# The shared keys by Strassen's seven products, in a float32 trunk of an mLSTM layer and a band-attention layer

## The chip, the cores and the metric

The kernel runs on one core of one Trainium2 chip. The metric is the device time of one execution in microseconds.

## The reference

512 tokens of width 2048 go through two layers. The first is an mLSTM mixer with eight heads, the second an attention mixer with sixteen heads of 128. Keys and values of the second layer are computed once, from the stream after the first layer:

```python
kmod = sc @ kv_ada_w.astype(F32) + kv_ada_b.astype(F32)
hkv = modulate(rmsnorm(x, kv_g), kmod[:, :D_MODEL], kmod[:, D_MODEL:]).astype(x.dtype)
kv = hkv @ kv_w
k_sh = kv[..., :B_WIDTH].reshape(Bn, S, B_HEADS, B_DH)
v_sh = kv[..., B_WIDTH:].reshape(Bn, S, B_HEADS, B_DH)
```

`hkv` is 512 x 2048, `kv_w` 2048 x 4096: one half of its columns gives the keys, the other the values. After that come the queries and a gate (`b_w_in`, 2048 x 4096), attention, and the output projection (`b_w_out`, 2048 x 2048). All is float32.

## The kernel before

Every float32 operand of a large product is held as a rounded half `hi` (type float32r) and a remainder `lo`. `split` makes them: ScalarE copies `hi` (line 153), VectorE subtracts for `lo` (line 154). A product of 128 x 128 weights with up to 512 tokens is then three matmuls, hi·hi, hi·lo, lo·hi (`mm3`); all of them are issued at line 174.

The weights lie in DRAM in the order in which they are used (`stream`). `wpiece` loads the next piece, as a rule 128 x 1024, into `wr` (tag `raw`, three buffers, line 167, on SP's queue like every DMA here) and splits it into `wh` and `wl` (three buffers each). From the end of the first stage on the pieces are issued with a priority of 300 instructions (`AHEAD`), so that they run ahead of the rest. The order on each engine and queue is fixed when the program is built: a list scheduler takes the ready instruction of the highest priority, and each engine then works in that order. A buffer is written again when its last reader is done.

`proj_a` makes one output tile of 128 columns by 512 tokens, with weights as the stationary operand: 16 k tiles, 48 matmuls, two pieces. `proj_b` makes tokens by 512 columns for several token tiles `m`, with the activations stationary.

The stages after the first layer are, in order:

- `rows`: the output projection of the first layer. Its input `y` is loaded from DRAM in pairs (`yr`, in the buffers of `raw`) and split (`y_tile`).
- `residual`, `turned`, `key_input`: the residual, its transposes (kept in DRAM in `nsc`), and `hkv` as hi and lo in the 16 buffers of `xp`.
- `values(g, ms)` for column groups 0 and 1, each for two pairs of token tiles (`PAIRS`). ScalarE copies the sums (`ps_kv`) to `kv[h]` in SBUF in pieces of 128 x 128 (line 685).
- The keys: 16 calls of `proj_a` with sums `ps_k`, copied to `kv[h]` (line 697).
- `values` for groups 2 and 3. While they run, `h2`, the input of the queries, is made from `nsc` into `xp` in place of `hkv`.
- Attention. Step `h` holds `queries(h)` (`ps_q`), `mixed(h - 2)` (`ps_o`), `weights(h - 1)` (`ps_s` and softmax), `gated(h)` (`ps_z`) and `flipped(h - 1)` (`ps_t`). `mixed` splits its output into `y2` in SBUF, in the buffers of `kp`.
- The output projection (`ps_y`), four column groups of `proj_b` over `y2`, and the last residual with `x2`, which is loaded into `xp` (line 813).

Of the kernel before, what the change touches and what calls it, by code (L numbers as in the profile page):

```python
# [9 lines left out]
F32 = mybir.dt.float32  # L10
# [5 lines left out]
P = 128  # L16
D = 2048
# [21 lines left out]
LATER += [DK, DK + P, V0 // 2 + DK, V0 // 2 + DK + P]  # L39


def stream():

    out = []

    def tile_a(mat, col, kts=KT):
        for k in range(0, kts, 8):
            out.append((mat, list(range(k, k + 8)), [(col, P)]))

    def tile_b(mat, col, kts=KT):  # L50
        for k in range(0, kts, 2):
            out.append((mat, [k, k + 1], [(col, 512)]))

    for k0, k1 in BLOCKS:
        for k in range(k0, k1):
            out.append(("a_w_in", [k], [(c, P) for c in LEAD]))
        for c in LATER:
            out.append(("a_w_in", list(range(k0, k1)), [(c, P)]))
    for h in range(NH):
        if h > 1:  # L60
            for c in (h * DK, h * DK + P, V0 // 2 + h * DK, V0 // 2 + h * DK + P):
                tile_a("a_w_in", c)
        tile_b("a_w_in", V0 + h * DV)
        if h:
            for c0 in (O0, Z0):
                for i in range(4):
                    tile_a("a_w_in", c0 + h * DV + i * P)
    tile_b("a_w_out", 0, 32)
    for _ in PAIRS:
        for g in range(1, 4):  # L70
            tile_b("a_w_out", g * 512, 32)
    for _ in PAIRS:
        for g in range(2):
            tile_b("kv_w", D + g * 512)
    for i in range(KT):
        tile_a("kv_w", i * P)
    for g in range(2, 4):
        tile_b("kv_w", D + g * 512)
    for h in range(BH):
        tile_a("b_w_in", h * P)  # L80
        tile_a("b_w_in", D + h * P)
    for g in range(3):
        tile_b("b_w_out", g * 512)
    for _ in PAIRS:
        tile_b("b_w_out", 3 * 512)
    return out


def sizes():
    return [len(kts) * sum(n for _, n in cs) for _, kts, cs in stream()]  # L90


CB = 0
# [12 lines left out]
def hybrid_trunk(ctx, tc, xT, xN, c, adaT, cols, wst, wg, ext, kc, out):  # L106
# [2 lines left out]

    const = ctx.enter_context(tc.tile_pool(name="const", bufs=1))  # L110
    dram = ctx.enter_context(tc.tile_pool(name="scr", bufs=1, space=bass.MemoryType.DRAM))
    wp = ctx.enter_context(tc.tile_pool(name="wp", bufs=3))
    xp = ctx.enter_context(tc.tile_pool(name="xp", bufs=KT))
    psP = ctx.enter_context(tc.tile_pool(name="psP", bufs=5, space=bass.MemoryType.PSUM))
    psA = ctx.enter_context(tc.tile_pool(name="psA", bufs=3, space=bass.MemoryType.PSUM))

    def pool(name, bufs=1):
        return tc.tile_pool(name=name, bufs=bufs, reuse_waits="tile")

    ysc = dram.tile([NH, P, 4, S], F32, name="ysc")  # L120
    gsc = dram.tile([2, NH, S], F32, name="gsc")
# [1 line left out]
    nsc = dram.tile([KT, P, S], F32, name="nsc")  # L123
    ggd = dram.tile([2, KT, P], F32, name="ggd")
    bsc = dram.tile([BH, P, EXTW], F32, name="bsc")

    cl = const.tile([P, NCOL], F32, name="cl")
    kcs = const.tile([P, 272], F32, name="kcs")
    ones_f = const.tile([P, P], F32, name="ones_f")
    ones_r = const.tile([P, P], F32R, name="ones_r")  # L130
# [8 lines left out]
    nc.vector.memset(ones_r.bitcast(F32), 1.0)  # L139
# [4 lines left out]
    maskd = kcs[:, 128:256]  # L144
    sel = kcs[:32, 256:272]

    def col(i):
        return cl[:, i : i + 1]
# [6 lines left out]

    ahead = [0]

    def wpiece(mat):

        i, at = wpos  # L160
        m, kts, cs = order[i]
        assert m == mat
        n = len(kts) * sum(w for _, w in cs)
        wpos[:] = i + 1, at + P * n
        with tc.high_priority(ahead[0]):
            raw = wp.tile([P, 1024], F32, tag="raw", name=f"wr{i}")[:, :n]
            nc.sync.dma_start(raw, wst[at : at + P * n].rearrange("(p n) -> p n", p=P))
            hi = wp.tile([P, 1024], F32R, tag="hi", name=f"wh{i}")[:, :n]
            lo = wp.tile([P, 1024], F32R, tag="lo", name=f"wl{i}")[:, :n]
            split(hi, lo, raw)  # L170
        return hi, lo

    def mm(ps, a, b, start, stop):
# [21 lines left out]
    def proj_b(mat, xs, pss, ms=range(4), kts=KT, at={}, late=0):  # L195


        held = []
        for k0 in range(0, kts, 2):
            if k0 in at:  # L200
                at[k0]()
            held.append((k0, *wpiece(mat)))
            if k0 >= kts - 2 * late and k0 < kts - 2:
                continue
            for group in [[pm] for pm in zip(pss, ms)] if k0 == kts - 2 else [list(zip(pss, ms))]:
                for ka, hi, lo in held:
# [7 lines left out]
            held.clear()  # L214

    def newp(name):
        return psP.tile([P, S], F32, tag="p", name=name)
# [46 lines left out]
    for q in range(4):  # L264
# [6 lines left out]
    pin(nc.sync.dma_start(kcs, kc))  # L271
# [63 lines left out]

    hp = hst.enter_context(pool("head"))
    aT = hp.tile([P, 4, NH], F32, name="aT")
    graw = tp.tile([P, KT, 16], F32, tag="t", name="graw")
    gw = hp.tile([P, KT, 32], F32R, tag="p0", name="gw")
    nc.sync.dma_start(graw, wg)  # L340
# [217 lines left out]

    kst = ExitStack()
    kp = kst.enter_context(pool("kp", bufs=KT))  # L560
    rst = ExitStack()
    rp = rst.enter_context(pool("rp", bufs=12))
    tst = ExitStack()
    tp = tst.enter_context(pool("t2", bufs=6))

    ys = []

# [107 lines left out]
            rows(g, ms, ys, at)  # L675


    kv = [kp.tile([P, 2, S], F32, tag="k", name=f"kv{h}") for h in range(BH)]
# [11 lines left out]
    for pair, ms in enumerate(PAIRS):  # L690
        for g in range(2):
            turn = {4 * i: lambda i=i: turned(1, [i], True) for i in range(4)} if pair == 0 and g == 1 else {}
            values(g, ms, turn)
    for i in range(KT):
        ps = newp(f"ps_k{i}")
        proj_a("kv_w", hkv, ps)
        nc.scalar.copy(kv[i][:, 0, :], ps)
    for g in range(2, 4):
        values(g, range(4))
    h2 = []  # L700
    for k in range(KT):
# [6 lines left out]
        h2.append(t)  # L708
    tst.close()
    rst.close()  # L710


    ast = ExitStack()
    at = ast.enter_context(pool("att"))
    y2 = []

    def queries(h):
        ps = newp(f"ps_q{h}")
        proj_a("b_w_in", h2, ps)
        q0 = at.tile([P, P], F32, tag="q0", name=f"q0_{h}")  # L720
# [71 lines left out]
    for h in range(BH + 2):  # L792
# [15 lines left out]
    yo = [[] for _ in range(4)]  # L808
    x2 = []
    for m in range(4):  # L810
        t = [xp.tile([P, 2, S], F32, tag="x", name=f"x2_{m}_{i}") for i in range(2)]
        for i in range(2):
            nc.sync.dma_start(t[i], xsc[m, :, 2 * i * S : 2 * (i + 1) * S].rearrange("p (a t) -> p a t", a=2))
        x2.append([t[g // 2][:, g % 2, :] for g in range(4)])

    def finish(m):
        rs = row_rstd(m)
# [5 lines left out]
    for g in range(4):  # L823
        gate_row(1, g)
        for pair in [range(4)] if g < 3 else PAIRS:
            ps = [newp(f"ps_y1_{g}_{m}") for m in pair]
            at = {4: lambda: finish(0), 6: lambda: finish(1)} if pair == PAIRS[1] else {}
            proj_b("b_w_out", y2, ps, ms=pair, at=at, late=3 if pair == PAIRS[1] else 0)
# [11 lines left out]
def layouts(x, c, ada_w, ada_b, g_pre, g_post, a_w_in, a_conv_w, a_conv_b, a_gate_b, a_g_head,  # L840
# [3 lines left out]
    def cc(v):  # L844
# [12 lines left out]
    order = stream()  # L857
    wst = np.concatenate(
        [
            np.concatenate([mats[mat][k * P : (k + 1) * P, c0 : c0 + n] for k in kts for c0, n in cs], 1).ravel()  # L860
            for mat, kts, cs in order
        ]
    )
    wg = np.ascontiguousarray(a_w_in[0][:, G0:].reshape(KT, P, 16).transpose(1, 0, 2))
# [3 lines left out]
    kc = np.zeros((P, 272), f)  # L868
    kc[:, :128] = np.eye(P)
    i = np.arange(P)  # L870
    kc[:, 128:256] = np.where(i[None, :] >= i[:, None], 0.0, NEG)
    kc[:32, 256:272] = np.tile(np.eye(16), (2, 1))
# [20 lines left out]
```

## Time and profile before

| | |
|---|---|
| time, median of 3 runs | 2862.86 us (2862.17 to 2864.84) |
| profiled execution, its own time | 2862.53 us |
| its span in the trace | 2860.7 us |
| granted TensorE clock | 0.999 |
| instructions | 33028 |
| matmuls | 12770 |

In the rows of the profile, PE is TensorE's matmuls and PEld its weight loads, DVE is VectorE, ACT is ScalarE, SP is the engine whose queue issues the DMAs, L174 is line 174. `ps_k<-hkv,wh` names what an instruction writes and reads. An arrow behind an idle time names what ended it.

### The profile page before, as it was taken

The page shows a single profiled execution, that of the slowest core. Times are in us where ns is not written, and L with a number is a line of the kernel's source. Part 1 is how long each engine was busy: PE and PEld are TensorE (multiplying, and loading weights), DVE is VectorE, ACT ScalarE, POOL GpSimd, SP SyncE. Part 2 cuts the span into 40 slices and gives each one's busy share as a digit, 9 for nine tenths or more (in the row PEclk, how much of TensorE's full clock was granted, in tenths as well). Part 3 has the DMA queues.
Part 4 walks back from the last instruction along what each step waited for, and adds up shares of the span by engine and source line. Part 5 has one row for each costly group of instructions (what it writes and reads, how often), then busy time and mean ns, then how long its engine had stood idle before and what let it go on. Part 6 is the DMA issues. An engine that isn't in the chain of part 4 may idle for free.

```text
span 2860.7 us, 33028 instructions
## 1 busy us (share of the span) xinstructions
PE 2832.2 (99%) x12770; PEld 2340.4 (82%) x12770; DVE 1587.4 (55%) x2358; ACT 1126.1 (39%) x1646; POOL 0.2 (0%) x4
## 2 busy tenths in 40 slices
PE   7999999999999999999999999999999999999998
PEld 5787888888888888888888888888888888888887
DVE  7986747466375564764735445575222455545425
ACT  4244524333242342332424345454222445545323
POOL 0000000000000000000000000000000000000000
PEclk9999999999999999999999999999999999999999
DMA  8874546456456464554635557786222322222334
GB/s 307 310 235 159 192 158 211 168 173 209 155 184 213 136 225 155 195 203 154 209 108 177 180 195 238 231 274 217 96 99 103 138 92 86 90 91 88 137 103 173
DMA packets 154950, 491.09 MB, mean 172 GB/s; under 512 B 17012, under 2 KB 26132, under 8 KB 154280
## 3 DMA queue, kind: packets, MB, share of 16 engines
q1 hardware_dynamic: 154792, 488.98, 50.2%
q8 instruction: 100, 1.64, 0.2%
q14 instruction: 58, 0.48, 0.0%
HBM read 467.89 MB, written 26.26 MB: 173 GB/s over the span
## 4 chain that ended last, share of the span: by engine, by line
PE 93%; DVE 3%; DMA 2%; issue 1%; ACT 1%; SPq 0%; DVEq 0%; ACTq 0%
PE ps_y L174 17%; PE ps_z L174 17%; PE ps_o L174 12%; PE ps_v L174 12%; PE ps_qk L174 9%; PE ps_q L174 6%; PE ps_k L174 6%; PE ps_kv L174 5%; PE ps_l L174 2%; PE ps_s L174 2%; PE ps_n L174 2%; PE ps_lead L174 1%; DVE wl L154 1%; DVE ada L245 1%; DMA wr<-in_wst 1%
## 5 line engine op out<-in xcount | busy, mean ns | idle before, releaser
L154 DVE TENSOR_TENSOR wl<-wr,wh 128x1024 fp32r<-128x1024 f32 (+3 forms) x586 | 680.4, 1162 | 1078.1 <-ACT wh L153 1077.6
L153 ACT CAST wh<-wr 128x1024 fp32r<-128x1024 f32 (+3 forms) x586 | 587.3, 1003 | 1433.0 <-PE ps_y L174 235.6
L174 PE MATMUL ps_y<-wh,y 128*128 128x512 f32 x1536 | 475.2, 390 | 0.0
L174 PE MATMUL ps_z<-h,wh 128*128 128x512 f32 x1408 | 433.9, 389 | 0.0
L174 PEld LDWEIGHTS ps_y<-wh,y 128*128 128x128 f32 x1536 | 288.2, 188 | 59.2
L174 PE MATMUL ps_v<-wh,h 128*128 128x512 f32 x1024 | 317.2, 389 | 0.0
L174 PEld LDWEIGHTS ps_z<-h,wh 128*128 128x128 f32 x1408 | 263.3, 188 | 54.0
L174 PE MATMUL ps_y<-wl,y 128*128 128x512 f32 x768 | 299.1, 389 | 0.0
L174 PE MATMUL ps_o<-h,wh 128*128 128x512 f32 x896 | 276.2, 389 | 0.0
L174 PE MATMUL ps_z<-h,wl 128*128 128x512 f32 x704 | 274.1, 389 | 0.0
L174 PE MATMUL ps_qk<-h,wh 128*128 128x512 f32 x768 | 237.8, 391 | 0.0
L174 PEld LDWEIGHTS ps_v<-wh,h 128*128 128x128 f32 x1024 | 192.1, 188 | 39.8
L174 PE MATMUL ps_v<-wl,h 128*128 128x512 f32 x512 | 199.4, 390 | 0.0
L174 PEld LDWEIGHTS ps_o<-h,wh 128*128 128x128 f32 x896 | 167.3, 188 | 34.1
L245 DVE CUSTOM_DVE_ANT_0 ada<-ada,scB,mod 128x1024 f32<-128x1024 f32 x128 | 164.1, 1282 | 24.2 <-DMA ada<-in_adaT 22.7
L174 PE MATMUL ps_o<-h,wl 128*128 128x512 f32 x448 | 174.4, 389 | 0.0
L174 PEld LDWEIGHTS ps_y<-wl,y 128*128 128x128 f32 x768 | 144.2, 188 | 30.0
L245 DVE CUSTOM_DVE_ANT_0 ada<-ada,scB,cl 128x1024 f32<-128x1024 f32 x128 | 164.0, 1282 | 6.0 <-DMA ada<-in_adaT 5.9
L174 PEld LDWEIGHTS ps_qk<-h,wh 128*128 128x128 f32 x768 | 143.2, 188 | 29.1
L174 PE MATMUL ps_q<-h,wh 128*128 128x512 f32 x512 | 159.3, 392 | 0.0
L174 PE MATMUL ps_kv<-wh,hkv 128*128 128x512 f32 x512 | 159.2, 391 | 0.0
L174 PE MATMUL ps_k<-hkv,wh 128*128 128x512 f32 x512 | 157.5, 389 | 0.0
(216 smaller groups left out, 3389.0 us busy)
## 6 DMA issues: line engine op xcount, KB each, us to landing
wr<-in_wst SPq DMA_DIRECT2D x520, 512.0 KB, 3.3
ada<-in_adaT SPq DMA_DIRECT2D x256, 512.0 KB, 5.4
yr<-ysc SPq DMA_DIRECT2D x16, 512.0 KB, 3.6
wr<-in_wst SPq DMA_DIRECT2D x30, 256.0 KB, 4.5
ysc<-so SPq DMA_DIRECT2D x28, 256.0 KB, 5.3
wr<-in_wst SPq DMA_DIRECT2D x16, 384.0 KB, 5.4
bsc<-in_ext SPq DMA_DIRECT2D x16, 320.0 KB, 6.1
xt<-in_xT SPq DMA_DIRECT2D x4, 1024.0 KB, 7.0
```

The source lines that it names most:

```text
L153: nc.scalar.copy(hi, src)
L154: nc.vector.tensor_tensor(lo, src, hi.bitcast(F32), op=ALU.subtract)
L174: nc.tensor.matmul(ps, a, b, start=start, stop=stop)
L245: pin(nc.vector.tensor_tensor_reduce(at, at, scB[:, j * D // 2 : (j + 1) * D // 2], 1.0, mod[:, i : i + 1] if j else col(CB + i), ALU.mult ...
```

## The change

The keys' output tiles are made in pairs. For two output tiles (columns `c1`, `c2`), two k tiles and two halves of 256 tokens, the eight products of 2 x 2 blocks become Strassen's seven, in the form with shared sums. Four PSUM banks `D`, `C`, `A`, `B` take them, half banks for single products, and VectorE puts the result `z` together from them at the end. The weights' sums are made in `wpiece` from the raw piece and split into buffers of their own (`ws`, `wsh`, `wsl`, two each); the tokens' sums (`half_sums`, called by `key_sums`) are made once for each pair of k tiles, from a modulated copy loaded from `nsc`. Four of the eight are made during the values before the keys, two during each of the first two output pairs. An output pair uses Strassen's form for the k pairs whose sums are there (`KEY_PAIRS`) and the plain eight products for the rest.

To make room, keys and values go to DRAM (`ksc`, `vsc`) and are fetched head by head in attention; the attention output goes to DRAM too (`y2c`) and is loaded and split in the output projection (`y2_tile`); `x2` is loaded into the buffers of `kp`. The pool of the weight buffers lies on the other side of SBUF, and some constants have moved to the first layer's pool.

```diff
+KEY_PAIRS = [4, 6, 8, 8, 8, 8, 8, 8]
+
+def pair_pieces(f):
+    sk, nk = list(range(f)), list(range(f, KT // 2))
+    n = min(len(sk), len(nk))
+    out = [([a], [b]) for a, b in zip(sk, nk)]
+    out[1:1] = [([], nk[i : i + 2]) for i in range(n, len(nk), 2)]
+    return out + [(sk[i : i + 2], []) for i in range(n, len(sk), 2)]
...
-    for i in range(KT):
-        tile_a("kv_w", i * P)
+    for i in range(KT // 2):
+        tile_s("kv_w", 2 * i * P, (2 * i + 1) * P, KEY_PAIRS[i])
...
-    wp = ctx.enter_context(tc.tile_pool(name="wp", bufs=3))
+    wp = ctx.enter_context(tc.tile_pool(name="wp", bufs=3, side="right"))
...
-    def wpiece(mat):
+    def wpiece(mat, ns=0, pl=None, bufs=2):
...
             nc.sync.dma_start(raw, wst[at : at + P * n].rearrange("(p n) -> p n", p=P))
+            out = []
+            if ns:
+                w = ns * P
+                t = pl.tile([P, 3 * w], F32, tag="ws", name=f"ws{i}", bufs=2)
+                nc.vector.tensor_tensor(t[:, : 2 * w], raw[:, w : 3 * w], raw[:, : 2 * w], op=ALU.subtract)
+                nc.vector.tensor_tensor(raw[:, w : 2 * w], t[:, w : 2 * w], raw[:, :w], op=ALU.add)
+                nc.vector.tensor_tensor(t[:, 2 * w :], raw[:, 3 * w : 4 * w], raw[:, w : 2 * w], op=ALU.subtract)
             hi = wp.tile([P, 1024], F32R, tag="hi", name=f"wh{i}")[:, :n]
             lo = wp.tile([P, 1024], F32R, tag="lo", name=f"wl{i}")[:, :n]
             split(hi, lo, raw)
+            if ns:
+                sh = pl.tile([P, 3 * w], F32R, tag="wsh", name=f"wsh{i}", bufs=bufs)
+                sl = pl.tile([P, 3 * w], F32R, tag="wsl", name=f"wsl{i}", bufs=bufs)
+                split(sh, sl, t)
+                return hi, lo, sh, sl
...
+    def proj_s(mat, xs, ss, f, z, name, pl, bufs, at={}):
+        D, C, A, B = [newp(f"ps_{n}{name}") for n in "dcab"]
...
+            def seven():
+                end = i == len(pieces) - 1
+                for ps, cols, b0, x, xcols, last in (
+                    (D, h1_, ns, lambda k: ss[k][1], h0, False),
+                    (D, h0, 0, lambda k: xs[2 * k], h0, end),
+                    (C, h0, -2 * ns, lambda k: ss[k][0], h1_, False),
+                    (C, h1_, -3 * ns, lambda k: ss[k][0], h0, end),
+                    (A, h0, 3 * ns, lambda k: xs[2 * k + 1], h0, False),
+                    (A, h1_, -ns, lambda k: xs[2 * k + 1], h1_, end),
+                    (B, h0, 2 * ns, lambda k: ss[k][1], h1_, end),
+                ):
+                    if i == 0 and ps is B:
+                        eight()
+                    for j, k in enumerate(sk):
+                        acc(ps, cols, b0 + j, x(k), xcols, last and j == ns - 1)
...
+        with tc.high_priority(AHEAD):
+            nc.scalar.copy(z[:, 0, :], D[:, h0])
+            nc.vector.tensor_tensor(z[:, 3, :], z[:, 0, :], D[:, h1_], op=ALU.add)
+            nc.vector.tensor_tensor(
+                z[:, 1:3, :], z[:, 3:4, :].to_broadcast([P, 2, 256]), C.rearrange("p (a t) -> p a t", a=2), op=ALU.add
+            )
+            nc.vector.tensor_tensor(z[:, 3, :], z[:, 1, :], C[:, h1_], op=ALU.add)
+            nc.vector.tensor_tensor(z[:, 0:2, :], z[:, 0:2, :], A.rearrange("p (a t) -> p a t", a=2), op=ALU.add)
+            if f < KT // 2:
+                nc.vector.tensor_tensor(z[:, 2:4, :], z[:, 2:4, :], B.rearrange("p (a t) -> p a t", a=2), op=ALU.add)
+            else:
+                nc.vector.tensor_tensor(z[:, 2, :], z[:, 2, :], B[:, h0], op=ALU.add)
+
+    def half_sums(raw, tmp, pl, tag, name):
+        (a11, a21), (a12, a22) = ((r[:, :256], r[:, 256:]) for r in raw)
+        (s1, s3), (s2, s4) = ((t[:, :256], t[:, 256:]) for t in tmp)
+        nc.vector.tensor_tensor(s1, a21, a22, op=ALU.add)
+        nc.vector.tensor_tensor(s3, a11, a21, op=ALU.subtract)
+        nc.vector.tensor_tensor(s2, a22, s3, op=ALU.subtract)
+        nc.vector.tensor_tensor(s4, a12, s2, op=ALU.subtract)
...
+            split(s[:, 0, :], s[:, 1, :], t)
...
-        for p, m in zip(pv, ms):
-            for j in range(4):
-                nc.scalar.copy(kv[4 * g + j][:, 1, m * P : (m + 1) * P], p[:, j * P : (j + 1) * P])
+        for i, (p, m) in enumerate(zip(pv, ms)):
...
+            nc.scalar.copy(v, p)
+            nc.sync.dma_start(vsc[g][:, :, m * P : (m + 1) * P], v.rearrange("p (j t) -> p j t", j=4))
...
+            if pair:
+                turn = {k: lambda k=k: key_sums(2 * g + k // 8) for k in (4, 12)}
             values(g, ms, turn)
-    for i in range(KT):
-        ps = newp(f"ps_k{i}")
-        proj_a("kv_w", hkv, ps)
-        nc.scalar.copy(kv[i][:, 0, :], ps)
+    rst.close()
+    zst = ExitStack()
+    zp = zst.enter_context(pool("zp", bufs=2, side="right"))
+    for i in range(KT // 2):
+        z = zp.tile([P, 4, 256], F32, tag="z", name=f"zk{i}")
+        ready = len(hs)
+        at = {j: lambda: key_sums(len(hs)) for j in (1, 2)} if ready < KT // 2 else {}
+        assert ready == KEY_PAIRS[i]
+        proj_s("kv_w", hkv, hs, ready, z, f"k{i}", zp, 2, at)
+        nc.sync.dma_start(ksc[i].rearrange("p a t -> p (a t)"), z.rearrange("p a t -> p (a t)"))
...
+    def fetch(h):
+        t = kp.tile([P, 2, S], F32, tag="k", name=f"kv{h}")
+        nc.sync.dma_start(t[:, 0, :], ksc[h // 2][:, h % 2, :])
+        nc.sync.dma_start(t[:, 1, :], vsc[h // 4][:, h % 4, :])
+        kv.append(t)
...
-        t = kp.tile([P, 2, S], F32R, tag="k", name=f"y2_{h}")
-        split(t[:, 0, :], t[:, 1, :], sz)
-        y2.append(t)
+        nc.sync.dma_start(y2c[h // 2][:, h % 2, :], sz)
...
-        t = [xp.tile([P, 2, S], F32, tag="x", name=f"x2_{m}_{i}") for i in range(2)]
+        t = [kp.tile([P, 2, S], F32, tag="k", name=f"x2_{m}_{i}") for i in range(2)]
...
+    def y2_tile(k):
+        while len(y2) <= k:
+            i = len(y2) // 2
+            raw = wp.tile([P, 2, S], F32, tag="raw", name=f"y2r{i}")
+            nc.sync.dma_start(raw, y2c[i])
+            for j in range(2):
+                t = xp.tile([P, 2, S], F32R, tag="x", name=f"y2_{i}_{j}")
+                split(t[:, 0, :], t[:, 1, :], raw[:, j, :])
+                y2.append(t)
+        return y2[k]
```

More of the change, by code (lines that the diff above doesn't have):

```diff
@@ L39, with add, tile_s @@
 LATER += [DK, DK + P, V0 // 2 + DK, V0 // 2 + DK + P]
+KEY_PAIRS = [4, 6, 8, 8, 8, 8, 8, 8]
[5 more added lines that the diff above has]
+    return out + [(sk[i : i + 2], []) for i in range(n, len(sk), 2)]
 def stream():
     out = []
+    def add(mat, kts, cs):
+        out.append((mat, [(k, c, n) for k in kts for c, n in cs]))
     def tile_a(mat, col, kts=KT):
         for k in range(0, kts, 8):
-            out.append((mat, list(range(k, k + 8)), [(col, P)]))
+            add(mat, range(k, k + 8), [(col, P)])
     def tile_b(mat, col, kts=KT):
         for k in range(0, kts, 2):
-            out.append((mat, [k, k + 1], [(col, 512)]))
+            add(mat, [k, k + 1], [(col, 512)])
+    def tile_s(mat, c1, c2, f):
+        for sk, nk in pair_pieces(f):
+            blocks = [(2 * k + i, c, P) for i, c in ((0, c1), (0, c2), (1, c2), (1, c1)) for k in sk]
+            out.append((mat, blocks + [(2 * k + i, c, P) for k in nk for i in range(2) for c in (c1, c2)]))
     for k0, k1 in BLOCKS:
         for k in range(k0, k1):
-            out.append(("a_w_in", [k], [(c, P) for c in LEAD]))
+            add("a_w_in", [k], [(c, P) for c in LEAD])
         for c in LATER:
-            out.append(("a_w_in", list(range(k0, k1)), [(c, P)]))
+            add("a_w_in", range(k0, k1), [(c, P)])
     for h in range(NH):
@@ L86, in stream @@
     return out
-def sizes():
-    return [len(kts) * sum(n for _, n in cs) for _, kts, cs in stream()]
 CB = 0
@@ L115, in hybrid_trunk, with pool @@
     psA = ctx.enter_context(tc.tile_pool(name="psA", bufs=3, space=bass.MemoryType.PSUM))
-    def pool(name, bufs=1):
-        return tc.tile_pool(name=name, bufs=bufs, reuse_waits="tile")
+    def pool(name, bufs=1, **kw):
+        return tc.tile_pool(name=name, bufs=bufs, reuse_waits="tile", **kw)
+    wp = ctx.enter_context(tc.tile_pool(name="wp", bufs=3, side="right"))
     ysc = dram.tile([NH, P, 4, S], F32, name="ysc")
@@ L125, in hybrid_trunk @@
     bsc = dram.tile([BH, P, EXTW], F32, name="bsc")
+    ksc = [dram.tile([P, 2, S], F32, name=f"ksc{i}") for i in range(BH // 2)]
+    vsc = [dram.tile([P, 4, S], F32, name=f"vsc{g}") for g in range(4)]
+    y2c = [dram.tile([P, 2, S], F32, name=f"y2c{i}") for i in range(BH // 2)]
     cl = const.tile([P, NCOL], F32, name="cl")
-    kcs = const.tile([P, 272], F32, name="kcs")
+    kcs = const.tile([P, 144], F32, name="kcs")
     ones_f = const.tile([P, P], F32, name="ones_f")
-    ones_r = const.tile([P, P], F32R, name="ones_r")
     cst = const.tile([P, 4], F32, name="cst")
@@ L143, in hybrid_trunk @@
     ident = kcs[:, 0:128]
-    maskd = kcs[:, 128:256]
-    sel = kcs[:32, 256:272]
+    sel = kcs[:32, 128:144]
     def col(i):
@@ L156, in hybrid_trunk @@
     ahead = [0]
-    def wpiece(mat):
+    def wpiece(mat, ns=0, pl=None, bufs=2):
         i, at = wpos
-        m, kts, cs = order[i]
+        m, blocks = order[i]
         assert m == mat
-        n = len(kts) * sum(w for _, w in cs)
+        n = sum(w for _, _, w in blocks)
         wpos[:] = i + 1, at + P * n
@@ L214, in proj_b, with acc, eight @@
             held.clear()
+    def proj_s(mat, xs, ss, f, z, name, pl, bufs, at={}):
+        D, C, A, B = [newp(f"ps_{n}{name}") for n in "dcab"]
+        pieces = pair_pieces(f)
+        begun = set()
+        h0, h1_ = slice(0, 256), slice(256, 512)
+        for i, (sk, nk) in enumerate(pieces):
+            if i in at:
+                at[i]()
+            ns = len(sk)
+            parts = wpiece(mat, ns, pl, bufs)
+            def acc(ps, cols, b, x, xcols, last):
+                start = id(ps) not in begun
+                begun.add(id(ps))
+                hi, lo = parts[:2] if b >= 0 else parts[2:]
+                w0 = (b if b >= 0 else b + 3 * ns) * P
+                w = slice(w0, w0 + P)
+                mm3(ps[:, cols], hi[:, w], lo[:, w], x[:, 0, xcols], x[:, 1, xcols], start, last)
+            def eight():
+                for m, k in enumerate(nk):
+                    for j in range(2):
+                        for t, ps in enumerate((A, B)):
+                            acc(ps, slice(0, S), 4 * ns + 4 * m + 2 * j + t, xs[2 * k + j], slice(0, S), False)
+            def seven():
[13 more added lines that the diff above has]
+                        acc(ps, cols, b0 + j, x(k), xcols, last and j == ns - 1)
+            if i:
+                eight()
+            seven()
+        with tc.high_priority(AHEAD):
[10 more added lines that the diff above has]
+                nc.vector.tensor_tensor(z[:, 2, :], z[:, 2, :], B[:, h0], op=ALU.add)
@@ new lines, in half_sums @@
+    def half_sums(raw, tmp, pl, tag, name):
[5 more added lines that the diff above has]
+        nc.vector.tensor_tensor(s4, a12, s2, op=ALU.subtract)
+        out = []
+        for i, t in enumerate(tmp):
+            s = pl.tile([P, 2, S], F32R, tag=tag, name=f"{name}_{i}")
+            split(s[:, 0, :], s[:, 1, :], t)
+            out.append(s)
+        return out
@@ L270, in hybrid_trunk @@
             pin(nc.sync.dma_start(cl, cols))
-    pin(nc.sync.dma_start(kcs, kc))
+    pin(nc.sync.dma_start(kcs, kc[:, :144]))
     early = [ada_load(KT, j, ap_, ADA_BUFS, pin) for j in range(2)]
@@ L337, in hybrid_trunk @@
     aT = hp.tile([P, 4, NH], F32, name="aT")
+    ones_r = hp.tile([P, P], F32R, name="ones_r")
+    nc.vector.memset(ones_r.bitcast(F32), 1.0)
+    maskd = hp.tile([P, P], F32, name="maskd")
+    nc.sync.dma_start(maskd, kc[:, 144:272])
     graw = tp.tile([P, KT, 16], F32, tag="t", name="graw")
@@ L560, in hybrid_trunk @@
     kp = kst.enter_context(pool("kp", bufs=KT))
+    tst = ExitStack()
+    tp = tst.enter_context(pool("t2", bufs=6, side="right"))
     rst = ExitStack()
-    rp = rst.enter_context(pool("rp", bufs=12))
-    tst = ExitStack()
-    tp = tst.enter_context(pool("t2", bufs=6))
+    rp = rst.enter_context(pool("rp", bufs=12, side="right"))
     ys = []
@@ L675, in hybrid_trunk @@
             rows(g, ms, ys, at)
-    kv = [kp.tile([P, 2, S], F32, tag="k", name=f"kv{h}") for h in range(BH)]
     def values(g, ms, at={}):
@@ L682, in values, with key_sums @@
         proj_b("kv_w", hkv, pv, ms=ms, at=at)
-        for p, m in zip(pv, ms):
-            for j in range(4):
-                nc.scalar.copy(kv[4 * g + j][:, 1, m * P : (m + 1) * P], p[:, j * P : (j + 1) * P])
+        for i, (p, m) in enumerate(zip(pv, ms)):
+            if g < 2:
+                v = tp.tile([P, S], F32, tag="t", name=f"v{g}_{m}")
+            else:
+                if i % 2 == 0:
+                    z = zp.tile([P, 2, S], F32, tag="z", name=f"v{g}_{m}")
+                v = z[:, i % 2, :]
+            nc.scalar.copy(v, p)
+            nc.sync.dma_start(vsc[g][:, :, m * P : (m + 1) * P], v.rearrange("p (j t) -> p j t", j=4))
+    hs = []
+    def key_sums(k):
+        raw = [kept(2 * k + i, slice(0, S)) for i in range(2)]
+        for i, r in enumerate(raw):
+            c = KT + 2 * k + i
+            nc.scalar.activation(r, r, AF.Identity, bias=mod[:, 80 + c : 81 + c], scale=amul[:, c : c + 1])
+        tmp = [tp.tile([P, S], F32, tag="t", name=f"hs{k}_{i}") for i in range(2)]
+        hs.append(half_sums(raw, tmp, kp, "k", f"hs{k}"))
     with tc.high_priority(AHEAD):
@@ L708, in hybrid_trunk @@
         h2.append(t)
+    zst.close()
     tst.close()
-    rst.close()
     ast = ExitStack()
     at = ast.enter_context(pool("att"))
-    y2 = []
+    kv = []
+    def fetch(h):
[3 more added lines that the diff above has]
+        kv.append(t)
+    fetch(0)
     def queries(h):
+        if h < BH - 1:
+            fetch(h + 1)
         ps = newp(f"ps_q{h}")
@@ L814, in hybrid_trunk @@
         x2.append([t[g // 2][:, g % 2, :] for g in range(4)])
+    y2 = []
+    def y2_tile(k):
[3 more added lines that the diff above has]
+            nc.sync.dma_start(raw, y2c[i])
+            for j in range(2):
+                t = xp.tile([P, 2, S], F32R, tag="x", name=f"y2_{i}_{j}")
+                split(t[:, 0, :], t[:, 1, :], raw[:, j, :])
+                y2.append(t)
+        return y2[k]
     def finish(m):
@@ L827, in hybrid_trunk @@
             at = {4: lambda: finish(0), 6: lambda: finish(1)} if pair == PAIRS[1] else {}
-            proj_b("b_w_out", y2, ps, ms=pair, at=at, late=3 if pair == PAIRS[1] else 0)
+            proj_b("b_w_out", y2_tile, ps, ms=pair, at=at, late=3 if pair == PAIRS[1] else 0)
             with tc.high_priority(AHEAD):
@@ L859, in layouts @@
         [
-            np.concatenate([mats[mat][k * P : (k + 1) * P, c0 : c0 + n] for k in kts for c0, n in cs], 1).ravel()
-            for mat, kts, cs in order
+            np.concatenate([mats[mat][k * P : (k + 1) * P, c0 : c0 + n] for k, c0, n in blocks], 1).ravel()
+            for mat, blocks in order
         ]
@@ L870, in layouts @@
     i = np.arange(P)
-    kc[:, 128:256] = np.where(i[None, :] >= i[:, None], 0.0, NEG)
-    kc[:32, 256:272] = np.tile(np.eye(16), (2, 1))
+    kc[:32, 128:144] = np.tile(np.eye(16), (2, 1))
+    kc[:, 144:272] = np.where(i[None, :] >= i[:, None], 0.0, NEG)
     return {
```

1 line of the change is left out of this document (removed).

## The prediction

> **What bounds the kernel now.** I read the busy times first, then the chain of waits, then the stages by windows.
>
> ```profile
> PE 2832.2 (99%) x12770; PEld 2340.4 (82%) x12770; DVE 1587.4 (55%) x2358; ACT 1126.1 (39%) x1646; POOL 0.2 (0%) x4
> ...
> PE 93%; DVE 3%; DMA 2%; issue 1%; ACT 1%; SPq 0%; DVEq 0%; ACTq 0%
> ```
>
> TensorE is busy for 99% of the span and is 93% of the chain that ended last. A matmul removed shortens the run, provided that its successors are ready. The chain in order of time shows the stages around the keys:
>
> ```profile
> 1547.66 214.45 PE ps_y L174 x946
> ...
> 1941.41 47.88 PE ps_kv L174 x211
> 1989.28 174.08 PE ps_k L174 x768
> 2163.36 87.04 PE ps_kv L174 x384
> ...
> 2669.90 3.22 PE ps_y L174 x14
> 2673.54 1.98 PE ps_o L174 x11
> 2677.80 3.20 PE ps_y L174 x14
> 2681.11 1.62 PE ps_y L174 x7
> 2684.31 1.39 PE ps_y L174 x6
> 2686.34 1.82 PE ps_o L174 x11
> 2688.16 158.94 PE ps_y L174 x701
> ```
>
> The keys are one unbroken piece: 768 matmuls of 512 tokens in 174.08 us, 226.7 ns each. The windows give the other engines in that stage and in its neighbours (columns: length, then busy time of PE, PEld, DVE, ACT, POOL, then clock, DMA share, GB/s):
>
> ```profile
> 0.00:125.00 125.00, 108.08 (x428) 83.65 (x429) 104.21 (x181) 44.82 (x68) 0.20 (x4) 1.00 0.85 305
> 1896.79:1941.41 44.62, 43.65 (x206) 35.50 (x206) 36.92 (x63) 30.88 (x65) 0.00 (x0) 1.00 0.84 276
> 1941.41:1989.28 47.87, 47.87 (x212) 39.59 (x212) 28.04 (x34) 23.89 (x44) 0.00 (x0) 1.00 0.69 233
> 1989.28:2163.36 174.08, 174.08 (x770) 144.14 (x769) 39.20 (x32) 41.78 (x52) 0.00 (x0) 1.00 0.29 100
> 2283.04:2669.90 386.86, 386.86 (x1862) 323.27 (x1861) 209.06 (x487) 197.14 (x352) 0.00 (x0) 1.00 0.28 96
> 2669.90:2688.16 18.26, 18.26 (x95) 14.96 (x94) 13.09 (x32) 11.57 (x23) 0.00 (x0) 1.00 0.41 134
> ```
>
> In the keys' stage VectorE is busy for 39.2 of 174.1 us, ScalarE for 41.8, the DMA for 29%; the clock is full. Nothing but TensorE binds there, and there is much room beside it.
>
> **The matmuls that go.** Per pair of output tiles and pair of k tiles, the old form issues 2 x 2 x 3 = 12 matmuls of 512 tokens: 12 x 226.7 ns = 2.720 us. Strassen's form issues 7 x 3 = 21 of 256 tokens. Their price is seen where the first layer's scores are 256 wide (timeline of PE):
>
> ```profile
> 516.40 0.88 PE L174 MATMUL ps_s<-qk,qk 128*128 128x256 f32 x6
> 517.11 0.63 PE L174 MATMUL ps_o<-h,wh 128*128 128x512 f32 x2
> ```
>
> Six of them hold the array from 516.40 to 517.11, start to start: 0.71 us, 118.3 ns each, each with a weight load of its own, at a granted clock of 1.00. A block then costs 21 x 118.3 = 2.484 us and saves 0.236. The eight output pairs take 4, 6, 8, 8, 8, 8, 8, 8 of the eight k pairs that way, 58 of 64. The stage becomes 58 x 2.484 + 6 x 2.720 = 160.4 us: **13.7 us less**. The bounds: both starts are read to 0.01 us, so a matmul takes 115 to 121.7 ns and the gain is 17.7 to 9.6 us. Break-even lies at 2.720/21 = 129.5 ns.
>
> The Trainium skill ("TensorE: Matmul & The Clock Gate", Back-to-back issue gap) speaks against this: it says that weight load and matmul together set the spacing in a sustained stream, and gives about 81 ns at 128 columns and 131 ns at 512. Interpolated, an estimate, 256 columns cost 98 ns, so a block would cost 2.05 us against 1.57, and the 58 blocks would lose 28 us. The traced 226.7 and 118.3 ns disagree with it: here the cost is nearly all columns.
>
> **VectorE's and ScalarE's new work in the keys' stage.** The groups of instructions (busy, mean ns of one):
>
> ```profile
> L154 DVE TENSOR_TENSOR wl<-wr,wh 128x1024 fp32r<-128x1024 f32 x520 | 636.4, 1224 | 1072.0 <-ACT wh L153 1071.5
> L153 ACT CAST wh<-wr 128x1024 fp32r<-128x1024 f32 x520 | 547.7, 1053 | 1330.8 <-PE ps_y L174 235.6 <-PE ps_z L174 228.0 <-PE ps_v L174 153.6
> L154 DVE TENSOR_TENSOR y<-yr,y 128x512 fp32r<-128x512 f32 x32 | 20.7, 688 | 30.1 <-ACT y L153 30.0
> L153 ACT CAST wh<-wr 128x512 fp32r<-128x512 f32 x30 | 18.5, 621 | 53.6 <-PE ps_l L174 29.9 <-PE ps_lead L174 16.4 <-DMA wr<-in_wst 7.3
> L154 DVE TENSOR_TENSOR wl<-wr,wh 128x768 fp32r<-128x768 f32 x16 | 15.3, 958 | 0.6 <-ACT wh L153 0.6
> L153 ACT CAST wh<-wr 128x768 fp32r<-128x768 f32 x16 | 13.4, 836 | 27.9 <-PE ps_l L174 14.2 <-DMA wr<-in_wst 13.1 <-PE ps_lead L174 0.5
> L154 DVE TENSOR_TENSOR wl<-wr,wh 128x256 fp32r<-128x256 f32 x20 | 8.2, 420 | 4.1 <-ACT wh L153 4.1
> L745 DVE SCALAR_TENSOR_TENSOR s<-ps_s,bias 128x128 f32<-128x128 f32 x16 | 4.5, 282 | 3.6 <-PE ps_s L174 3.6
> L154 DVE TENSOR_TENSOR p<-e,p 128x384 fp32r<-128x384 f32 x8 | 4.4, 553 | 0.0
> ```
>
> A weight piece with two Strassen k pairs costs VectorE one sum of 512 (0.69), two of 256 (0.84), the old remainder of 1024 (1.22) and a new one of 768 (0.96): 3.71 us. One with a single pair and a plain one: 0.42 + 0.56 + 1.22 + 0.55 = 2.76. Putting an output pair together takes three operations of 512 and two of 256, 2.9 us, or two and three, 2.6, when all eight k pairs are Strassen's. A call of `key_sums` is four of 256 and two remainders of 512: 3.06. So pair 0 costs 4 x 2.76 + 2.9 + 2 x 3.06 = 20.1 us beside 20.8 of TensorE, pair 1 costs 22.0 beside 20.4, each later pair 17.5 beside 19.9. Together that is **147 us of VectorE in a stage of 160**, 92%, where it was 23%. ScalarE needs at most 1.05 + 0.84 a piece, some 70 us with copies and `key_sums`: covered.
>
> Whether VectorE delays TensorE is a matter of its lead. Weights have three buffers, the extra sums two, and both are filled with a priority of 300 instructions. The second buffer of sums comes free after 36 of a piece's 42 matmuls (4.3 of 5.0 us), and TensorE needs it 12 matmuls into the piece after next, some 7 us later, against 0.84 + 0.96 us of splitting. The new waits are those of the assembling operations on the last piece's four sums: with them VectorE stands between TensorE's groups of 1.4 us, and behind it queue the next pieces' splits. At most 4.3 us pass from the first group's end to the last's, with 2.6 us of work in them: 1.7 us idle per pair, and 17.5 + 1.7 still fits in 19.9. In the first two pairs the 42.1 us meet 41.2, but the last two `key_sums` feed k pairs 6 and 7, first read in the last piece of pair 2, so 1.5 us or so can slide there. I price stalls here at 2 us; the bounds are 0 and, if all idle of all eight pairs adds, 14.
>
> **The stage before the keys.** Four `key_sums` (12.2 us of VectorE) and the first pieces' extra sums (some 4 us) come into the window of 1941.41: 28.0 + 16 = 44 of 47.9 us, 92%. Its DMA gets eight loads and six stores of 256 KB, 3.7 MB more on 11.2: about 310 GB/s, what the first 125 us carry (305, at a share of 0.85). That first window and that of 1896.79 show the price of VectorE at 83%: 16.9 and 1.0 us of idle PE, the first of them at the kernel's start. I take 1 us, from the second as the nearer; bounds 0 and 4. The value copies are cheaper for ScalarE than before (four of 128 become one of 512).
>
> **The detour of keys, values and attention outputs through DRAM.** Sixteen value stores, eight key stores, 32 fetches, 16 `y2c` stores and eight loads, all on SP's queue with the weights. In attention (0.28, 96 GB/s) this adds 16 x 0.75 MB over 387 us, about 32 GB/s: nothing, under TensorE's 386.86 of 386.86. A store that waits for its data holds the weight loads behind it, but the weights have three raw buffers of 5.4 us of matmuls each.
>
> **The handover to the output projection.** Until now `y2` lay in SBUF, and TensorE filled the last head's softmax with `ps_y`: the four listed pieces between 2669.90 and 2686.34 are 41 matmuls, 9.4 us of the 18.26 us window. Now each `y2` pair needs a load, two buffers that `h2` leaves while `ps_z` of the last head runs, and four splits of 0.62 to 0.69 us. There were idle stretches for the first ones:
>
> ```profile
> 2668.77 1.04 ACT L153 CAST wh<-wr 128x1024 fp32r<-128x1024 f32 x1 [3.67 <-issue]
> 2669.85 1.23 DVE L154 TENSOR_TENSOR wl<-wr,wh 128x1024 fp32r<-128x1024 f32 x1 [3.61 <-ACT wh L153]
> ```
>
> Inside the window VectorE goes from 13.1 us to at most 13.1 + 6 x 0.69 = 17.2 of 18.3, less what fits into those stretches. I take 1.5 us; bounds 0 and 9.4. After that the scheme of load and split is that of `yr` in the first layer's output projection, which ran without a gap (946 matmuls in 214.45 us, 226.7 ns each). `x2` moves to earlier buffers: nothing. The moved constants (a 64 KB load behind the start pool, one buffer side changed) have no row; I take 0, bounds -1 and 2.
>
> **Sum.** The profiled execution took 2862.53 us (span 2860.7 and 1.8 around it); the median is 0.3 above it. 2862.5 - 13.7 + 2 + 1 + 1.5 = **2853 us**.
>
> **The rivals.** (1) *VectorE becomes the bound of the keys' stage.* For: in the two fullest windows above it was at 83% when TensorE began to starve; at 83%, 147 us of work take 177 us, 2.9 longer than today's 174.1, and with 2.5 at entry and handover the run takes **2868**. Against: those windows have DMA at 0.84 and long chains, the keys' stage has neither. It decides from 147/174, that is if VectorE can't be kept busier than 84%. Chance 0.2. (2) *The handover or the entry eats the gain:* `y2` comes so late that the 9.4 us of fill wait until the softmax is over: 2853 - 1.5 + 9.4 = **2861**, no measurable change. For: VectorE's 17.2 of 18.3 us. Against: the first splits have idle engines before the window. Chance 0.16. (3) *Weight loads stop overlapping in long runs.* One lasts 144.14 us / 769 = 187 ns in the keys' stage, the spacing of six matmuls is 118.3; were that only a lead used up by six, a block would cost 21 x 187 = 3.93 us, the 58 blocks 70 us more than now, and the run **2933**. It decides from 129.5 ns. The skill's rule above is of this kind. Against: no spacing in the row of six shows it, and six is more than one spare weight buffer explains. Chance 0.04.
>
> **How the numbers follow.** 0.6 for the forecast, whose own range is 2846 (115 to 116 ns and few stalls) to 2857. 0.2 per cent, 5.7 us, is what a measurement of this kernel tells from no change. Faster 0.6; same 0.16; slower 0.24, from rivals 1 and 3. The range runs from 2846 to 2868, which leaves out rival 3 and the tails.
>
> **What would show it.** `ps_k` is replaced by four sums whose matmuls start 118 ns apart, the stage about 162 to 163 us long; VectorE at 90% in it; no idle of PE over 1 us that `wl` or the extra sums end. A stage over 174 us with PE waiting for VectorE is rival 1; `ps_y` idle after 2650 us is rival 2; an even spacing over 129 ns is rival 3.

## The result and the profile after

The changed kernel takes 2857.57 us (median of 8 runs, 2853.95 to 2861.16), the kernel before 2863.6 us in the same series: ratio 0.9976, 95% interval 0.9967 to 0.9985. It is faster by 0.24%, some 6 us. The profiled execution took 2857.92 us, 4.6 less than that of before.

Page of the changed kernel, busy times and chain by engine:

```profile
PE 2823.8 (99%) x13292; PEld 2357.8 (83%) x13292; DVE 1690.6 (59%) x2574; ACT 1158.5 (41%) x1654; POOL 0.2 (0%) x4
...
PE 91%; DVE 3%; DMA 3%; ACT 1%; issue 1%; SPq 0%; DVEq 0%; ACTq 0%
```

TensorE still binds. The chain in order of time gives the pace inside the keys and the places of what follows:

```profile
2027.35 1.44 PE ps_dk L205 x12
2028.79 1.44 PE ps_ck L205 x12
2030.22 1.44 PE ps_ak L205 x12
...
2158.39 87.07 PE ps_kv L205 x384
2245.45 10.88 PE ps_q L205 x48
```

Twelve matmuls of 256 tokens take 1.44 us, 120 ns each. The second values begin at 2158.39 where they began at 2163.36: 5.0 us have been won by then, and little changes after that. The windows of the same stages as before, the keys' stage (1989.90 to 2158.39) also in three parts:

```profile
1896.30:1941.90 45.60, 43.84 (x204) 35.26 (x203) 35.95 (x60) 30.71 (x58) 0.00 (x0) 1.00 0.86 274
1941.90:1989.90 48.00, 48.00 (x218) 39.69 (x216) 36.72 (x59) 31.27 (x44) 0.00 (x0) 1.00 0.78 261
1989.90:2010.50 20.60, 20.60 (x129) 18.37 (x128) 15.12 (x33) 11.61 (x18) 0.00 (x0) 1.00 0.66 213
2010.50:2035.00 24.50, 20.65 (x138) 19.11 (x137) 23.26 (x43) 13.76 (x20) 0.00 (x0) 0.93 0.61 207
2035.00:2158.39 123.39, 123.39 (x1030) 123.39 (x1029) 98.53 (x153) 44.47 (x54) 0.00 (x0) 1.00 0.47 159
1989.90:2158.39 168.49, 164.64 (x1291) 160.87 (x1290) 136.91 (x226) 69.84 (x91) 0.00 (x0) 0.99 0.51 173
...
2278.09:2665.08 386.99, 386.99 (x1862) 323.30 (x1861) 199.89 (x477) 191.71 (x342) 0.00 (x0) 1.00 0.35 111
2665.08:2683.55 18.47, 18.47 (x95) 15.23 (x95) 15.71 (x37) 13.73 (x28) 0.00 (x0) 1.00 0.41 144
```

The keys take 168.5 us for 174.1. All of TensorE's idle time in the stage, 3.85 us, lies in one part of 24.5 us, where VectorE is at 95% and the granted clock falls to 0.93. From 2035 on TensorE is never idle, with VectorE at 80%. The timeline shows what happens at 2011 (engine, line, operation, and in brackets the idle time and what ended it):

```profile
2011.59 1.52 ACT L806 ACTIVATE xt<-xt,mod,amul 128x512 f32<-128x512 f32 x2
...
2013.01 0.35 ACT L294 COPY zk<-ps_dk 128x256 f32<-128x256 f32 x1
...
2014.19 0.42 DVE L310 TENSOR_TENSOR hs<-xt,xt 128x256 f32<-128x256 f32 x1
2014.53 0.41 DVE L295 TENSOR_TENSOR zk<-zk,ps_dk 128x256 f32<-128x256 f32 x1
...
2014.99 0.50 PE L205 MATMUL ps_ck<-hs,wsh 128*128 128x256 f32 x2 [3.14 <-DVE zk L295]
...
2016.68 0.77 PE L205 MATMUL ps_ak<-hkv,wh 128*128 128x256 f32 x2 [0.71 <-DVE zk L299]
```

The second pair's first product into `C` waits 3.14 us. Its weights are there. What is missing is a PSUM bank: five banks rotate over four sums per pair, so the second pair's `C` needs the bank of the first pair's `D`, and that is emptied late. ScalarE copies half of `D` at 2013.01, behind two activations of a key sum; VectorE adds the other half at 2014.53, behind a row of sums. The next wait, 0.71 us, is `A` for the bank of the first pair's `C`. The windows right behind show the clock:

```profile
2015.00:2018.00 3.00, 2.29 (x12) 2.11 (x13) 3.00 (x7) 1.98 (x3) 0.00 (x0) 0.70 0.70 259
2018.00:2021.00 3.00, 3.00 (x12) 2.46 (x12) 3.00 (x5) 2.26 (x3) 0.00 (x0) 0.73 0.63 224
2021.00:2024.00 3.00, 3.00 (x17) 2.50 (x16) 3.00 (x7) 1.68 (x2) 0.00 (x0) 1.00 0.35 126
```

These means of 0.70 and 0.73 come from one stretch at half clock, from 2016.2 to 2019.6:

```profile
2016.20:2019.60 3.40, 2.92 (x10) 2.66 (x11) 3.40 (x7) 2.50 (x4) 0.00 (x0) 0.50 0.44 167
```

TensorE is busy for 2.92 of these 3.40 us, so the half clock costs 2.92 x 0.5 = 1.5 us beside the idle time.

### The profile page after: what moved, and what is told of

The parts are those of the page before. It is cut to its first block, busy times and chain, and to the rows that moved or that the text cites. A ratio compares the mean times of both kernels' runs of the same rounds, so it can differ in the third digit from the quotient of the medians.

```text
span 2856.1 us, 34604 instructions
## 1 busy us (share of the span) xinstructions
PE 2823.8 (99%) x13292; PEld 2357.8 (83%) x13292; DVE 1690.6 (59%) x2574; ACT 1158.5 (41%) x1654; POOL 0.2 (0%) x4
## 4 chain that ended last, share of the span: by engine, by line
PE 91%; DVE 3%; DMA 3%; ACT 1%; issue 1%; SPq 0%; DVEq 0%; ACTq 0%
PE ps_z L205 17%; PE ps_y L205 17%; PE ps_o L205 12%; PE ps_v L205 12%; PE ps_qk L205 9%; PE ps_q L205 6%; PE ps_kv L205 3%; PE ps_l L205 3%; PE ps_s L205 2%; PE ps_n L205 2%; DMA wr<-in_wst 2%; PE ps_lead L205 2%; PE ps_ak L205 2%; PE ps_ck L205 1%; PE ps_dk L205 1%; DVE wl L172 1%
## 5 line engine op out<-in xcount | busy, mean ns | idle before, releaser
L205 PEld LDWEIGHTS ps_o<-h,wh 128*128 128x128 f32 x896 | 167.3, 188 | 34.2
L205 PEld LDWEIGHTS ps_z<-h,wl 128*128 128x128 f32 x704 | 132.2, 188 | 27.7
```

Source lines behind the costliest of these rows:

```text
L205: nc.tensor.matmul(ps, a, b, start=start, stop=stop)
```

## The experiments

The theory to test: the products pay nearly as computed, at 120 ns for 118.3, and the rest of the expected gain is lost to the order in which the first pair's banks are emptied, with a lowered clock behind it. Its rivals: VectorE's load, late loads from DRAM, or a costly detour that hides a larger gain. The verdicts below rest on the keys' stage of each trace, since run to run a whole execution varies by several us. Each version has one trace, so a stage's time is a single sample.

**A bank to spare for D.**

```diff
-        D, C, A, B = [newp(f"ps_{n}{name}") for n in "dcab"]
+        D, C, A, B = [(newa if n == "d" else newp)(f"ps_{n}{name}") for n in "dcab"]
```

> Edit: the sum D of each pair of key tiles comes from the three attention banks of PSUM, which are idle in this stage; A, B and C keep the other five. Theory (bank wait): in the changed kernel the second pair's first product into C starts 3.1 us late and its first into A 0.7 us late because VectorE empties the first pair's D and C late, and the granted clock then stays at about 0.7 for 6 us (1.7 us more). With a bank to spare all of that goes: the keys' stage shrinks from 168.5 to about 163 us, the run to about 2852, ratio to before 0.996. Rival (VectorE is full): VectorE is at 95% from 2010 to 2035 us, so the stall only moves to a wait for a split weight or for split sums; stage within 1.5 us of 168.5, run about 2857.

Measured: 2855.99 us, ratio 0.997 (0.9958 to 0.9982). The windows of the stage, of the stall and of what follows it:

```profile
1991.90:2156.10 164.20, 162.66 (x1290) 159.37 (x1290) 135.47 (x223) 69.91 (x91) 0.00 (x0) 1.00 0.52 176
2015.00:2018.50 3.50, 1.96 (x9) 1.30 (x8) 3.50 (x9) 2.68 (x5) 0.00 (x0) 1.00 0.71 277
2018.50:2026.00 7.50, 7.50 (x50) 6.85 (x49) 7.50 (x14) 4.41 (x7) 0.00 (x0) 1.00 0.45 152
```

The stage shrinks by 4.3 us. The waits for `C` and `A` are gone, and with them the low clock: behind the 1.5 us that remain it stays at 1.00. What remains is a wait for a bank again, the first pair's `C`:

```profile
PE ps_bk L205 <- DVE zk L299: 1.5, 1, 1.5
```

VectorE is full here too, and no wait for a weight or a key sum took the stall's place. So a bank was what TensorE lacked, whatever VectorE's load; the expected 163 us were missed by what was left of the wait. Whether the bank came free late by the order of the operations or by their amount, this run can't tell.

**The detour alone.** Keys as before by `proj_a`, no sums; everything else of the change stays.

```diff
-        proj_s("kv_w", hkv, hs, ready, z, f"k{i}", zp, 2, at)
+        for j in range(2):
+            ps = newp(f"ps_k{i}_{j}")
+            proj_a("kv_w", hkv, ps)
+            nc.scalar.copy(z[:, 2 * j : 2 * j + 2, :].rearrange("p a t -> p (a t)"), ps)
```

> Edit: keys by the plain 768 matmuls of 512 again and no sums at all; the detour of keys, values and attention outputs through DRAM, the moved pools and x2 stay. Theory: the detour costs under 1 us, so the run is within 1.5 us of before (2862 to 2865), with a keys' stage of 174 us. Rival: the detour costs 3 us or more (late splits at the handover, DMA in the values' stages) and hides a larger gain of the products: 2866 or more.

Measured: 2864.43 us, ratio 1.0003 (0.9994 to 1.0012); the keys' stage is 173.8 us again:

```profile
1989.90:2163.70 173.80, 173.80 (x769) 143.90 (x768) 42.47 (x38) 41.42 (x48) 0.00 (x0) 1.00 0.49 165
```

The interval reaches from 1.7 us won to 3.4 us lost, so whole executions show no clear cost of the detour through DRAM, the moved pools and `x2`. In the traces, what lies behind the keys takes 697.8 us (2861.5 - 2163.7) for 697.3 (2860.7 - 2163.36). A detour that hides a gain larger than 3.4 us is not there.

**One key sum per pair.** `KEY_PAIRS = [4, 5, 6, 7, 8, 8, 8, 8]`, and `key_sums` at the second piece only.

> Edit: key sums are made one per output pair, not two, over the first four pairs; Strassen's form takes 4, 5, 6, 7, 8, 8, 8, 8 of the k pairs, 54 blocks for 58. Theory (backlog of VectorE and ScalarE in the first two pairs delays the emptying of the banks): with 3 us of VectorE less in pairs 0 and 1 the 3.9 us of idle and the low clock behind it mostly go, against 0.8 us for the four blocks: 2853 to 2855. Rival (order, not load: the copy of D stands behind activations of the key sums on ScalarE whatever their number): the stall stays within 1 us and the run is at 2858 or above.

Measured: 2858.71 us, ratio 0.9978 (0.9969 to 0.9987), its keys' stage 170.0 us. Waits and windows:

```profile
PE ps_ck L205 <- DVE zk L295: 2.2, 1, 2.2
PE ps_ak L205 <- DVE zk L299: 0.7, 1, 0.7
```

```profile
1992.60:2162.60 170.00, 167.07 (x1255) 160.81 (x1254) 134.20 (x227) 68.86 (x90) 0.00 (x0) 0.98 0.50 171
2014.40:2018.50 4.10, 1.40 (x10) 0.99 (x8) 4.10 (x11) 3.02 (x6) 0.00 (x0) 0.94 0.59 200
2018.50:2026.00 7.50, 7.27 (x24) 6.10 (x25) 5.96 (x13) 3.12 (x6) 0.00 (x0) 0.58 0.48 170
```

Three microseconds less of VectorE in each of the first two pairs take 0.9 us off the wait, not the wait itself. The half clock lasts twice as long:

```profile
2018.00:2024.80 6.80, 6.09 (x18) 5.08 (x18) 6.46 (x14) 3.13 (x5) 0.00 (x0) 0.50 0.59 214
```

The traced execution took 2862.09 us, more than the median, but the median's ratio is no better than the changed kernel's either. The theory in this form, that a lighter first two pairs cures the stall, is wrong. The order is what is left to explain the late bank; it is read from the timeline, and no run changed it alone.

**All key sums early.** `KEY_PAIRS = [8] * 8`; `key_sums` at four places of each of the two value groups before the keys.

> Edit: all eight key sums are made during the values before the keys, so that all 64 blocks take Strassen's form and the keys' stage holds no key sums. VectorE then has about 49 us of work in the 48 us before the keys. Theory: the keys' stage has no bank wait (about 161.5 us for 64 blocks at 120 ns a matmul), but the stage before it loses several us to VectorE and DMA: the keys start 3 to 8 us later than at 1989.7, run 2852 to 2858. Rival (the entry hides it, as it hid four): keys start within 1 us of 1989.7, run about 2850.

Measured: 2863.01 us, ratio 0.9995 (0.9986 to 1.0004): the gain is gone. Windows of the stage before the keys, of the keys, and of a part of them:

```profile
1941.90:1991.40 49.50, 49.50 (x224) 40.91 (x223) 39.49 (x63) 34.26 (x49) 0.00 (x0) 1.00 0.81 272
1991.40:2163.70 172.30, 165.64 (x1346) 164.14 (x1345) 141.64 (x225) 70.90 (x89) 0.00 (x0) 0.98 0.49 165
1999.50:2013.00 13.50, 7.00 (x45) 5.50 (x43) 13.02 (x27) 9.78 (x15) 0.00 (x0) 0.96 0.42 143
```

Of TensorE's waits in the keys, the largest group is this:

```profile
PE ps_ck L205 <- ACT hs L171: 3.0, 2, 1.8
```

The place was expected wrongly. The stage before the keys loses nothing; VectorE carries what it can't do there into the first keys, and TensorE waits for key sums (3.0 us in the row above) and loses 6.5 us in 13.5, VectorE being busy for 13.0 of them. Most of a wait of 1.4 us for a bank that ScalarE's copy of the values holds lies in it too. Here VectorE's load does cost time, and the change's split of four, two and two avoids it.

**Two whole sets of sums.** As the first experiment, with `n in "db"`: `D` and `B` in the attention banks, `C` and `A` in the other five.

> Edit: D and B of each pair from the three attention banks, C and A from the other five, so that two whole sets of sums fit into PSUM. Theory: with D alone moved, the second pair's first product into B still waited 1.7 us for the bank of the first pair's C; that goes too. Keys' stage from 164.3 to about 162.5 us at a full clock (58 blocks of 21 matmuls of 120 ns and 6 of 2.72 us make 162.5), no idle of PE over 0.3 us in it, run about 2853.5 to 2855. Rival (VectorE's backlog comes due elsewhere): a wait for wl, wsl or a key sum of 1 us or more takes its place, stage 164 us or more.

Measured: **2853.24 us, ratio 0.9958 (0.9944 to 0.9971)**, the fastest version. Its keys' stage:

```profile
1992.70:2156.20 163.50, 162.87 (x1291) 159.51 (x1290) 136.27 (x227) 70.26 (x91) 0.00 (x0) 1.00 0.53 178
```

TensorE's wait in it:

```profile
PE ps_bk L205 <- DVE zk L295: 0.6, 1, 0.6
```

0.6 us of idle are left, a wait of `B` for `D`'s bank; the rest is matmuls at 120 ns. This is what the products are worth: 10.6 us of keys (174.1 - 163.5). VectorE's 136.3 us are 83% of it, so at that share TensorE does not starve.

**Loads of the key sums first.** The changed kernel with `kept` inside `tc.high_priority(AHEAD)` in `key_sums`.

> Edit: the changed kernel with the loads of the key sums issued at the weights' priority, earlier on SP's queue; in its program the copy of the first pair's D then stands behind all four key sums of pairs 0 and 1 on ScalarE, where in the changed kernel it stood behind three. Rival theory (late loads): the backlog of ScalarE and VectorE in pair 0 comes from a wait of 5.7 us for a load from nsc; loaded in time, the bank waits of 3.9 us fall under 1 us, stage about 163.5, run about 2853. My theory (order on ScalarE and VectorE): the emptying of D still comes behind the key sums and PE still waits 2 us or more for the bank; stage 166 us or more, run 2856 or more.

Measured: 2856.37 us, ratio 0.9972 (0.9961 to 0.9983), the stage 167.3 us.

```profile
1990.40:2157.70 167.30, 164.53 (x1292) 160.97 (x1291) 136.76 (x225) 69.00 (x90) 0.00 (x0) 0.99 0.52 173
...
PE ps_ck L205 <- DVE zk L295: 2.3, 1, 2.3
```

TensorE still waits 2.3 us for the same bank. Late loads were not the main cause, though earlier ones take about 0.8 us off the wait.

**One and two more sums per piece.** The two-set version with the line `nc.vector.tensor_tensor(t[:, : 2 * w], ...)` of `wpiece` two and three times.

> Edit: e5_two_sets with the first sum of each Strassen weight piece made twice on VectorE (one operation of 512 or 256 more in each of 32 pieces, 20 us). VectorE then has 157 us of work in a stage of 162.5, 97%. My theory (VectorE can be filled to the end, its lead covers the rest): stage under 166 us. Rival 1 of the prediction (above some 84% of VectorE TensorE starves): stage 157/0.84 = 187 us, run about 2878.

> Edit: e5_two_sets with the first sum of each Strassen weight piece made three times (40 us more). VectorE has 177 us of work where TensorE has 162.5. Both theories: VectorE is the bound now. Mine: stage 171 to 178 us, about VectorE's own 177 us less its lead at the start. Rival 1: 177/0.84 = 211 us.

Measured: 2858.6 us (ratio 0.9975, 0.9964 to 0.9985) and 2858.0 us (0.9977, 0.9967 to 0.9988). The keys' stages, first with one more, then with two:

```profile
1989.80:2154.80 165.00, 163.19 (x1291) 159.70 (x1290) 152.68 (x257) 70.61 (x89) 0.00 (x0) 1.00 0.52 174
```

```profile
1991.50:2158.50 167.00, 163.60 (x1289) 159.84 (x1290) 165.35 (x287) 70.54 (x91) 0.00 (x0) 1.00 0.51 170
```

At 152.7 of 165.0 us (93%) TensorE loses 1.8 us, at 165.4 of 167.0 (99%) 3.4. The rival that TensorE starves above 84% of VectorE, 187 and 211 us, is refuted. My own 171 to 178 for the second was too high as well, since it added up durations: two operations of VectorE that follow each other overlap. In the timeline of the changed kernel above, line 310 starts at 2014.19 and line 295 at 2014.53, 0.34 us apart, where each lasts 0.41 to 0.42. Why the one-more version's whole runs (2854.5 to 2861.2) are no faster than the two-more's, with a stage 2 us shorter, stays open. The traced execution of the one-more version took 2854.58 us for a median of 2858.6, so its trace may not show what the longer executions lose.

## Why the prediction was right, term by term

The sum was made against the profiled executions, 2862.53 and now 2857.92.

- *The matmuls.* Predicted 13.7 us less at 118.3 ns, bounds 9.6 to 17.7. A long run of them takes 120 ns: 58 x 21 x 0.120 + 16.3 = 162.5 us, **11.6 less**. The mechanism held, the term was 2.1 us too large: a price from six in a row, 118.3 ns, was carried to 1218. The rival that weight loads stop overlapping is refuted by the same rows. So is the loss that the Trainium skill's pair of figures for 128 and 512 columns gave for the 58 blocks ("TensorE: Matmul & The Clock Gate", Back-to-back issue gap): 226.7 and 120 ns are nearly in the proportion of the columns, the 120 being some 7 ns over the half.
- *Stalls in the keys' stage.* Predicted 2 us, bounds 0 to 14; it was 168.5 - 162.5 = **6.0**: 3.85 of idle, 1.5 of half clock, and some 0.7 of small change. This is the step that was mis-sized most, and in kind too. I had followed the lead of weights and sums through their buffers, and it holds: no piece waited for `wl` or for the extra sums. I had not followed the PSUM banks, five for four sums, nor seen that the assembling of one pair stands in the engines' orders behind key sums of the next. The two-set version shows it: with banks to spare the stage is 163.5 us, with the same load on VectorE. Nor did I have a price for a lowered clock: where TensorE is idle for 2.63 us in the first layer of before, its clock stays at 1.00.
- *VectorE's load.* Predicted 147 us, measured 136.9, or 81% and not 92%. The work was counted rightly: the durations of VectorE's operations in the stage add up to 148.9 us. But those of neighbours overlap.
- *The stage before.* Predicted 1 us. TensorE is never idle in that window (48.00 of 48.00 us). The keys' first matmul starts 0.5 us later than it did (1989.6 for 1989.1), but that is within the spread of executions: in the two-set version, which differs only behind this point, it starts at 1992.5. VectorE's 36.7 of 48.0 us are under the forecast 44, the DMA's 261 GB/s under 310.
- *Handover and detour.* Predicted 1.5 us. The last window has its 18.47 us of matmuls for 18.26, and VectorE 15.7 us, under the 17.2 allowed. From the second values to the end of the span the kernel loses 0.4 us: 2856.1 - 2158.39 against 2860.7 - 2163.36.

Together -11.6 + 6.0 + 0.5 + 0.4 = -4.7 us, against -4.6 measured; the 0.5 can't be told from spread. Forecast were -9.5. The median says -6.0, between the two; the changed kernel's runs spread over 7 us, those of before over 4. Whether the stall and the clock behind it are longer in some runs than in others would need more profiles; it stays open. The median of 2857.57 us lies just outside the forecast's own range of 2846 to 2857, and the 6.0 us are only just over the 5.7 that the prediction wanted to tell a gain from no change. So the way and the mechanism were right, and that the size fell inside the wide range of 2846 to 2868 is partly luck. That range held because its upper part was made for stalls of just this size, under another name: the rival had VectorE starve TensorE by load, and what came was a wait for a bank.

## What to carry to other kernels

Fewer, narrower matmuls paid here, though less than their columns say: a block has an eighth fewer columns and took 2.52 us for 2.72, 7% less. So count matmuls as well as columns, and take the price from a long run. When a stage gets more accumulators, follow the banks as carefully as the operand buffers: two whole sets of sums took 5 us off the stage, which a lighter load of VectorE in the first two pairs did not. Price VectorE's work by start-to-start times, and a stall of TensorE by its idle time plus the clock behind it.

## What the hardware showed

- At the first hand-over the granted clock fell to one half: for 3.4 us in the changed kernel, after 3.1 us of idle and 0.7 close behind, and for 6.8 us in the version with one key sum per pair, after 2.2 and 0.7. After 1.5 us, with a bank to spare for `D`, it stayed at 1.00. The Trainium skill ("TensorE: Matmul & The Clock Gate", Part 1) puts the danger at gaps of more than about 3.4 us; here less was enough. Nor does the length alone decide it. The same wait in the first layer, 2.6 to 2.7 us, left the clock of before at 1.00, while the changed kernel was at half clock from 67.2 to 70.6. The five matmuls behind it show this, first before, then after:

```profile
66.51 1.43 PE L174 MATMUL ps_lead<-h,wh 128*128 128x512 f32 x5 [2.63 <-ACT h L224]
...
67.54 2.50 PE L205 MATMUL ps_lead<-h,wh 128*128 128x512 f32 x5 [2.68 <-ACT h L329]
```

- VectorE ran at 99% of a stage of 167 us while TensorE lost 3.4 us.
- Weight loads of 192 ns each followed one another every 120 ns without a gap: PEld busy for 123.39 of 123.39 us, and the pace still went by the matmuls' columns: 226.7 ns at 512 and 120 at 256 make, as an estimate, 0.42 ns a column and some 13 ns more for each matmul.
